# A ring for the keys and other memory for chunks of y in a one-core hybrid block

## The chip, the cores and the metric

The kernel runs on one core of a Trainium2 chip. The metric is the device time of one execution in microseconds (us). The core's engines work side by side and meet only at semaphores: TensorE (PE; its weight loads are shown as PEld), VectorE (DVE), ScalarE (ACT), GpSimd (POOL) and SyncE (SP), which here issues most of the DMAs; POOL issues the others. SBUF is the on-chip memory for operands, PSUM the one that TensorE writes.

## The reference

One layer of an autoregressive decoder for 1024 positions of width 1024, in float32:

```python
mod = c @ w_ada + b_ada                       # shift, scale, gate
h = rmsnorm(x, norm_g) * (1 + scale) + shift
proj = h @ w_in     # q, k, v, g_attn, xr, g_rnn, m_attn, m_rnn
y_attn = sliding_window_attention_with_sinks(rope(q), rope(k), v, sinks) * silu(g_attn)
y_rnn = rg_lru(causal_depthwise_conv(xr), ...) * silu(g_rnn)
merged = sigmoid(m_attn) * (y_attn @ w_attn_proj) + sigmoid(m_rnn) * (y_rnn @ w_rnn_proj)
x = x + gate * (merged @ w_out)
out = rmsnorm(x, final_g)
```

The attention has 16 query heads in 4 groups, each group with one key and value head of width 64. A block of 128 queries sees its own block of 128 keys and the one before, under a band mask of 128 positions, plus one learned sink value per head.

## The kernel before

**Numbers.** Each float32 operand of a matmul is split into a high part, its copy rounded to the matmul's format, and a low part, the rest. A product is the sum of high x high, low x high and high x low. So keys are stored as two parts per block (the axis `b` of `k_d`), weights as `wh` and `wl`, and y as `yh` and `yl`.

**The block products.** `w_in` is applied in pairs of 128-column chunks. Each pair takes seven products of half size in place of eight (a Strassen-like scheme): class `Pair`, with the list of steps in `run`. One step is a slot: 12 matmuls of 512 columns on TensorE. A slot's products read the normalised x (`hh`, `hl`) or sums and differences of its quarters (high parts `nh`, low parts `nl`). `make_operands` makes four tiles `nl`, one for each i from 0 to 3, each of 128 partitions x 2 x 1024. Each tile holds four quarters of 512 columns, which different products read: `NT1` is the first half of row 0, `NT3` the second half of row 0, `NT4` the first half of row 1, `T2` the second half of row 1. There are 23 pairs. `s_last`, the first slot of the last pair, is 154. The last pair reads `NT1` in slot 155, `T2` in slot 157, the quarters of `hh` and `hl` with numbers 4 to 7 in slots 158 and 159, `NT3` in slot 160 and `NT4` in slots 156 and 161.

**Memory.** Pools of tiles are opened and closed in the manner of a stack, from the left and from the right. `hb` (`hh` and `hl` 4 to 7), `hx` (first x transposed, later `nl`), `hn` (`nh`) and `stp` belong to `h_ctx`, and this is closed when `rp_steps` begins; `ypool`, `tout` and `hpool` then take over their memory. A tile in such memory waits, before it is first written, for the tiles that lay there.

**The attention loop** (line 1720, at the end of `tile_hybrid_block`) runs over u = 0 to 34. Each turn starts unit u (a group's block of 128 queries, four heads) and carries on the units before it: scores and maxima of u, exponentials of u - 1, transposes of u - 2, values of u - 3. Between the scores of u and the transposes stands one piece of other TensorE work from the generator `fill`: in units 0 to 5 the last slots 156 to 161 of the block products, from unit 6 on the pieces of `rp_steps`. A piece is 12 matmuls in either case.

**`rp_steps`** is the product of y (the recurrent branch's output, eight chunks of 128 rows, in DRAM as `yh_d` and `yl_d`) with `w_rnn_proj`. Its first eight pieces are for the output chunks 0 and 1 and read y in this order: chunks 6 and 7 (units 6 and 7), 4 and 5 (units 8 and 9), 0 and 1 (units 10 and 11), 2 and 3 (units 12 and 13). After these all chunks are in SBUF and are read again for the output chunks 2 to 7.

**Loads of y** (`load_y`). Chunk 6 and the high part of chunk 7 were left in SBUF. The low part of chunk 7 and all of chunk 0 go into halves of `hh` and `hl` 0 to 3; they are asked for in slots 157 and 159. Chunks 4 and 5 are asked for at the start of `rp_steps`, chunks 1, 2 and 3 in its pieces 1, 2 and 3, all into `ypool` (12 tiles of 512 KB). One chunk is 1 MB: a high and a low half of 512 KB.

**Loads of keys and queries** (`load_kq`, line 1319). Units 2m and 2m + 1 make pair m. Its tile `ks` holds three blocks of keys (the one before and its own two; only two at the start of a group), 384 KB, and `qs` its queries, 512 KB. Two pools take turns. Pair 0 is loaded early, in the middle of the last gates' work (line 1068), pair 1 in `open_attn`, and pair m, from 2 on, behind the scores of unit 2m - 3, whose pool it takes over.

**Gates** (`load_gq`, line 1549). A pair's attention output is multiplied by its gate, 256 KB from `ga_d`, loaded into the same six buffers `r` that the weight halves of `w_rp` use (`load_r`). Gate m is asked for at the end of unit 2m + 2, and `a_prep` multiplies two or more units later: in `f1` on DVE, `f2` on ACT, `f3` on DVE.

**Order.** Up to `order.close()` each engine issues its instructions in the order in which the program writes them; `at_slot` puts steps behind a slot's product. So SP's queue is in that order too: a DMA that must wait, such as a store whose data are not ready, holds all DMAs behind it. Stores made within the loop are set aside in `behind` and issued by `flush` after the unit's piece. Behind `order.close()` the instructions are placed by the compiler's scheduler.

Of the kernel before, what the change touches and what calls it, by code (L numbers as in the profile page):

```python
# [13 lines left out]
F32R = mybir.dt.float32r  # L14
# [4 lines left out]
ALU = mybir.AluOpType  # L19
# [3 lines left out]
P = 128  # L23
# [32 lines left out]
def tile_hybrid_block(ctx, tc, x, pk, rows, posr, posi, c_row, w_ss, w_gate, w_main, w_v,  # L56
# [8 lines left out]
    def f32(ap):  # L65
        return ap.bitcast(F32)
# [75 lines left out]


    hba = ctx.enter_context(tc.tile_pool(name="hba", bufs=1))
    h_ctx = ExitStack()
    hb = h_ctx.enter_context(tc.tile_pool(name="hb", bufs=1))
    b12_ctx = ExitStack()
# [10 lines left out]
                lst.append([a[:, SL[0]], a[:, SL[1]]])  # L158
                full.setdefault(kc, []).append(a[:])
    xx = b12_ctx.enter_context(tc.tile_pool(name="xx", bufs=1, side="right"))  # L160
    hx = h_ctx.enter_context(tc.tile_pool(name="hx", bufs=4))
    xall = [hx.tile([P, 2, S], F32, tag="X", name="xT") for i in range(3)]
    xall.append(xx.tile([P, 2, S], F32, name="xT3"))
    xT = [xall[kc % 4][:, kc // 4, :] for kc in range(KC)]
# [390 lines left out]
    B11 = [(hh[i][0], hl[i][0]) for i in range(4)]  # L555
    B21 = [(hh[i + 4][0], hl[i + 4][0]) for i in range(4)]
    B22 = [(hh[i + 4][1], hl[i + 4][1]) for i in range(4)]
    NT1, NT3, NT4, T2 = [], [], [], []

    def differences(i):  # L560
        b11, b12_ = xT[i][:, SL[0]], xT[i][:, SL[1]]
# [476 lines left out]
    def after_gates(hb, oc):  # L1038
# [22 lines left out]
        def d2():  # L1061
            V.tensor_tensor(out=t["it"][:], in0=t["it"][:], in1=W["xc", hb, oc][2][:],
                            op=ALU.mult)
            W["used", hb, oc] = True
            if c == KC - 1:
                xc_ctx.close()
                W["kq", 0] = pool(at_ctx, "kq0", side="right")
                load_kq(0)

        def a3():  # L1070
            A.activation(tl("th"), t["rz"][:], AF.Tanh)
# [230 lines left out]
    def open_attn():  # L1302
        nonlocal at, psx
        psm_ctx.close()
        psx = pool(psx_ctx, "psx", space=PSUM)
        W["kq", 1] = pool(at_ctx, "kq1", side="right")
        W["pp"] = pool(at_ctx, "pp", bufs=3, side="right")
        W["pp"].tile([P, 64], F32, name="pad", bufs=1)
        W["neg"] = W["pp"].tile([P, 8], F32, name="neg", bufs=1)
        G.memset(W["neg"][:], -1e30)  # L1310
        for nm in ("vb", "hl", "yo"):
            W[nm] = pool(at_ctx, nm, side="right")
        at = pool(at_ctx, "at", side="right")
        load_kq(1)
        for u in range(4):
            load_v(u)
            load_d(u)

    def load_kq(m):
        g, t0 = m // 4, (m % 4) * 256  # L1320
        ks = W["kq", m % 2].tile([P, 3, 2, P], F32R, tag="ks", name="ks")
        kv = k_d.rearrange("(p j) n b t -> j p n b t", j=4)[g]
        n0 = t0 // P
        lo = 1 if t0 == 0 else 0
        dma(ks[:, lo:, :, :], kv[:, n0 - 1 + lo:n0 + 2, :, :])
        qs = W["kq", m % 2].tile([P, 4, 256], F32R, tag="qs", name="qs")
        dma(qs[:], q_d[g][m % 4].rearrange("(a j) t -> a j t", j=4))
        U["kq", m] = ks, qs

    def load_v(u):  # L1330
        vb = U["v", u] = W["vb"].tile([P, P], F32R, tag="vb", name="vb", bufs=5)
# [11 lines left out]

    def scores(u):
        g, n = u // 8, u % 8
        ks, qs = U["kq", u // 2]
        qc = slice((n % 2) * P, (n % 2 + 1) * P)
        kb = n % 2 + (0 if n else 1)
        s_full = psx.tile([P, 1024], F32, tag="s", name="s_ps")
        s_ps = s_full[:].rearrange("p (j k) -> p j k", j=4)  # L1350
        for j in range(4):
            o = s_ps[:, j, :] if n else s_ps[:, j, P:]
            for b in range(2):
                W["pe"] = T.matmul(o, qs[:, j, qc], ks[:, kb:n % 2 + 2, b, :],  # L1354
                                   start=(b == 0), stop=(b == 1))
        sm = W["pp"].tile([P, 2, 4], F32, tag="small", name="small", bufs=4)
        U["s", u] = s_ps, U.pop(("p", u)), sm

    def maxima_a(u):
        s_ps, px, sm = U["s", u]  # L1360
        A.copy(px[:, :, 0:P], s_ps[:, :, P:])

    def maxima_d(u):
        s_ps, px, sm = U["s", u]
        p = px[:, :, 0:P]
        V.copy_predicated(p, W["mgt"][:].unsqueeze(1).to_broadcast([P, 4, P]),
                          s_ps[:, :, 0:P] if u % 8 else
                          W["neg"][:, 0:1].unsqueeze(1).to_broadcast([P, 4, P]))
        V.tensor_reduce(out=sm[:, 0, :], in_=px[:], axis=AX.X, op=ALU.max, negate=True)

# [97 lines left out]
                todo.pop(0)()  # L1468

    def load_y(c):  # L1470
        if c == 0:
            yh[c], yl[c] = [[t[i][0] for i in range(2)] for t in (hh, hl)]
            for i in range(2):
                dma(yh[c][i], yh_d[c][:, SL[i]])
                dma(yl[c][i], yl_d[c][:, SL[i]])
            return
        if c >= 6:
            yh[c], yl[c] = [[y_in[c, b][:, t_] for t_ in SL] if (c, b) in y_in else
                            [hh[2 + i][0] for i in range(2)] for b in range(2)]
            if c == 7:  # L1480
                for i in range(2):
                    dma(yl[c][i], yl_d[c][:, SL[i]])
            return
        h_ = W["yp"].tile([P, S], F32R, tag="Y", name="yh")
        l_ = W["yp"].tile([P, S], F32R, tag="Y", name="yl")
        dma(h_[:], yh_d[c])
        dma(l_[:], yl_d[c])
        yh[c] = [h_[:, SL[0]], h_[:, SL[1]]]
        yl[c] = [l_[:, SL[0]], l_[:, SL[1]]]

    def rp_steps():
        h_ctx.close()
        pb_ctx.close()
        psr = pool(ps_ctx, "psr", space=PSUM, side="right")
        rp_acc.extend(psr.tile([P, S], F32, name=f"rp{i}") for i in range(2))
        W["yp"] = pool(ctx, "ypool", bufs=12)
        W["tout"] = pool(ctx, "tout", bufs=1)
        W["hpool"] = pool(ctx, "hpool", bufs=6)

        def part(c, kc2):  # L1500
            for kc in (2 * kc2, 2 * kc2 + 1):
                W["pe"] = mm_k([rp_acc[c % 2][:, t] for t in SL], (O.get((c, 0)), O.get((c, 1))),
                               kc, xh=yh, xl=yl, ends=(6, 3) if c < 2 else (0, KC - 1))

        def finish(c):
            def f():
                flush()
                t = W["tout"].tile([P, S], F32, tag="rp", name="rp32")
                A.copy(t[:], rp_acc[c % 2][:])
                store(tr_d[c], t[:])  # L1510
            later_a.append(f)
            if "att" not in W:
                do_later()

        seq = [(c, k) for k in (3, 2, 0, 1) for c in range(2)]
        seq += [(c, k) for c in range(2, KC) for k in range(4)]
        load_y(4)
        load_y(5)
        for i, (c, k) in enumerate(seq):
            part(c, k)  # L1520
            if i in (1, 2, 3):
                load_y(i)
            if i in (1, 2):
                prep_r(i - 1, 0)
            if i in (6, 10):
# [160 lines left out]
    while W["slot"] < 7 * (len(pairs) - N_ATT) + 1:  # L1686
# [2 lines left out]

    s_last = 7 * len(pairs) - 7  # L1690
    load_y(6)
    at_slot(s_last + 2, ("N", 0, 0, lambda: load_r(0)), ("N", 0, 0, lambda: load_y(7)),
            ("N", 0, 0, lambda: load_r(1)), ("N", 0, 0, lambda: load_y(0)),
            ("N", 0, 0, lambda: prep_r(0, 1)), ("N", 0, 0, lambda: prep_r(1, 1)))

    def fill():
# [23 lines left out]
    for u in range(32 + 3):  # L1720
# [42 lines left out]
        do_later()  # L1763
        if u >= 3 and u % 2 == 0:
            late.append((u - 3) // 2)
        if u >= 2 and len(loaded) < 16 and len(loaded) <= (u - 2) // 2 and (
                len(loaded) - (late[0] if late else (u - 2) // 2) < 2):
            m = len(loaded)
            load_gq(m)
            loaded[m] = u  # L1770
# [62 lines left out]
    for c in range(KC):  # L1833
# [26 lines left out]
            A.copy(h, t[:, LEFT])  # L1860
            V.tensor_tensor(out=l, in0=t[:, LEFT], in1=f32(h), op=ALU.subtract)
        else:
            mh, ml = [ypool.tile([P, S], F32R, tag="Y", name=n_) for n_ in ("mh", "ml")]
            for i in SL:
                A.copy(mh[:, i], t[:, i])
            V.tensor_tensor(out=ml[:], in0=t[:], in1=f32(mh[:]), op=ALU.subtract)
            A12.append((mh[:, LEFT], ml[:, LEFT]))
            A22.append((mh[:, RIGHT], ml[:, RIGHT]))
            a11, a21 = [raw[c - 4][:, i] for i in SL]
# [227 lines left out]
```

## Time and profile before

| | us |
|---|---|
| median of 3 runs | 909.88 |
| lowest and highest run | 909.71, 911.13 |
| the profiled execution | 909.71 |
| its span from first to last instruction | 908.0 |
| first attention unit to the last piece of `rp_steps` on TensorE | 557.9 to 745.7 |

The profile's page gives the busy time of each engine as a share of the span. A matmul's end is modelled, so a busy TensorE need not be at its peak. The chain of waits is followed back from the last instruction to whatever released it; a row has a start, a duration, an engine or a DMA, a tile and the line of the code. The windows give the busy time of each engine in a stretch, the TensorE clock that was granted (1.00 is full), the mean busy share of the 16 DMA engines, and what they moved. A row of the DMA view has the tiles, the issuing queue, the count, the size of one, and the median time from issue to landing.

### The profile page before, as it was taken

How to read it: one execution, taken by the hardware profiler on the slowest of the kernel's cores; microseconds unless marked ns; L12 is line 12 of the kernel's file. 1: busy time of each engine (PE TensorE's matmuls, PEld its weight loads, DVE VectorE, ACT ScalarE, POOL GpSimd, SP SyncE). 2: the span in 40 equal slices, each digit the busy share in tenths (PEclk: the TensorE clock that was granted, in tenths of full speed). 3: DMA queues.
4: the chain of work that ended last, by engine and by line, in shares of the span. 5: the costliest groups of instructions: out<-in, count | busy, mean ns of one | idle time of the engine just before them, and what ended most of it. 6: DMA issues, size and time to landing. Idle time of an engine off the chain costs nothing.

```text
span 908.0 us, 12850 instructions
## 1 busy us (share of the span) xinstructions
PE 892.6 (98%) x4314; PEld 747.0 (82%) x4315; DVE 718.5 (79%) x1063; ACT 569.8 (63%) x1099; POOL 186.8 (21%) x330
## 2 busy tenths in 40 slices
PE   9999999999999999999999999997999999999997
PEld 6789888888888888888888888886888888888786
DVE  6998697989679877897897696996999836578855
ACT  7965564655566865777686974885888732115535
POOL 6430241200000000000000002695887720000000
PEclk9999999999999999999999999998999999999999
DMA  9829489863542374265534347997887379416604
GB/s 360 332 94 284 146 258 294 273 212 128 196 163 105 128 251 144 101 229 165 202 112 167 124 137 227 298 344 193 245 237 221 114 263 362 139 47 232 209 1 185
DMA packets 93829, 179.79 MB, mean 198 GB/s; under 512 B 15506, under 2 KB 36002, under 8 KB 93764
## 3 DMA queue, kind: packets, MB, share of 16 engines
q1 hardware_dynamic: 82336, 164.44, 53.0%
q0 software_dynamic: 11280, 14.27, 5.7%
q8 instruction: 34, 0.56, 0.3%
q14 instruction: 31, 0.25, 0.1%
q10 hardware_dynamic: 148, 0.27, 0.1%
HBM read 121.60 MB, written 57.64 MB: 197 GB/s over the span
## 4 chain that ended last, share of the span: by engine, by line
PE 89%; DMA 4%; DVE 3%; ACT 2%; issue 1%; SPq 0%; ACTq 0%
PE bk L714 48%; PE rp L175 13%; PE pgate L1031 5%; PE out L1900 4%; PE pmain L175 4%; PE s_ps L1354 3%; PE pmain L487 2%; PE bk L487 2%; PE pv L1424 2%; DMA yh<-yh_d 2%; DMA qs<-q_d 1%; PE pt L1388 1%; DMA wo<-wo_d 1%; PE pmain L1603 1%; PE pmain L1601 1%; PE pmain L1602 1%
## 5 line engine op out<-in xcount | busy, mean ns | idle before, releaser
L714 PE MATMUL bk<-nh,wh 128*128 128x512 f32 x368 | 143.3, 389 | 0.0
L714 PE MATMUL bk<-nl,wh 128*128 128x512 f32 x368 | 143.2, 389 | 0.0
L714 PE MATMUL bk<-nh,wl 128*128 128x512 f32 x368 | 98.4, 389 | 0.0
L106 ACT CAST wh<-r 128x512 fp32r<-128x512 f32 x107 | 65.5, 618 | 34.1 <-PE pmain L175 10.4
L112 DVE TENSOR_TENSOR wl<-r,wh 128x512 fp32r<-128x512 f32 x91 | 62.1, 691 | 26.2 <-ACT wh L106 26.1
L714 PEld LDWEIGHTS bk<-nh,wl 128*128 128x128 f32 x368 | 69.1, 188 | 14.3
L714 PEld LDWEIGHTS bk<-nl,wh 128*128 128x128 f32 x368 | 69.1, 188 | 14.3
L714 PEld LDWEIGHTS bk<-nh,wh 128*128 128x128 f32 x368 | 69.1, 188 | 14.2
L63 POOL DMA_DIRECT2D yl_d<-it x1 | 0.6, 568 | 349.7 <-DVE it L1114 349.7
L714 PE MATMUL bk<-hl,wh 128*128 128x512 f32 x184 | 71.6, 389 | 0.0
L714 PE MATMUL bk<-hh,wh 128*128 128x512 f32 x184 | 71.6, 389 | 0.0
L112 DVE TENSOR_TENSOR wl<-ws,wh 128x512 fp32r<-128x512 f32 x76 | 51.8, 684 | 6.8 <-ACT wh L106 6.8
L106 ACT CAST wh<-ws 128x512 fp32r<-128x512 f32 x76 | 45.9, 615 | 8.4 <-DVE ws L736 4.1
L1374 ACT ACTIVATE p<-p,small 128x129 f32<-128x129 f32 x128 | 50.0, 396 | 0.0
L714 PE MATMUL bk<-hh,wl 128*128 128x512 f32 x184 | 49.2, 389 | 0.0
L1354 PE MATMUL s_ps<-ks,qs 128*128 128x256 f32 (+1 forms) x256 | 36.5, 286 | 5.2 <-DMA qs<-q_d 5.2
L714 PEld LDWEIGHTS bk<-hl,wh 128*128 128x128 f32 x184 | 34.6, 188 | 7.2
L714 PEld LDWEIGHTS bk<-hh,wl 128*128 128x128 f32 x184 | 34.5, 188 | 7.2
L714 PEld LDWEIGHTS bk<-hh,wh 128*128 128x128 f32 x184 | 34.5, 188 | 7.1
L1354 PEld LDWEIGHTS s_ps<-ks,qs 128*128 128x128 f32 x256 | 33.6, 195 | 6.8 <-issue 5.6
L175 PE MATMUL rp<-yh,wh 128*128 128x512 f32 x112 | 35.8, 402 | 0.0
L714 PE MATMUL bk<-hha,wh 128*128 128x512 f32 x92 | 35.8, 389 | 0.0
(379 smaller groups left out, 2385.3 us busy)
## 6 DMA issues: line engine op xcount, KB each, us to landing
r<-w_main SPq DMA_DIRECT2D x100, 256.0 KB, 4.3
wada<-w_ss SPq DMA_DIRECT2D x16, 512.0 KB, 9.0
qs<-q_d SPq DMA_DIRECT2D x16, 512.0 KB, 8.0
wo_d<-wr SPq DMA_DIRECT2D x28, 256.0 KB, 4.3
wo<-wo_d SPq DMA_DIRECT2D x14, 512.0 KB, 6.6
ks<-k_d SPq DMA_DIRECT2D x12, 384.0 KB, 6.2
xt<-x SPq DMA_DIRECT2D x8, 512.0 KB, 6.9
sma_d<-c SPq DMA_DIRECT2D x16, 256.0 KB, 4.2
```

The source lines that it names most:

```text
L106: A.copy(dst[0][:], src)
L112: eng.tensor_tensor(out=dst[1][:], in0=src, in1=f32(dst[0][:]), op=ALU.subtract)
L175: mm = T.matmul(ps[hf], ww, xx[kc][hf], start=(kc == ends[0] and ww is w_h and xx is xh), stop=(kc == ends[1] and xx is xl))
L487: T.matmul(starts[c][hf], ww[:, c0:c0 + P], xh[kc][hf], start=(kc == 0 and t_ == "h"), stop=(kc == KC - 1 and t_ == "l"))
L714: W["pe"] = T.matmul(ps, ww[:, kc * P:(kc + 1) * P], b[kc][i], start=(first and n == 0), stop=(n == 11), skip_group_check=not first)
L1031: W["pe"] = T.matmul(ps[:, SL[hf]], ww[:, c0:c0 + P], xx_[:, SL[hf]], start=(ic == 0 and i == 0), stop=(ic == 1 and i == 2))
L1354: W["pe"] = T.matmul(o, qs[:, j, qc], ks[:, kb:n % 2 + 2, b, :], start=(b == 0), stop=(b == 1))
L1374: A.activation(px[:, j, :], px[:, j, :], AF.Exp, bias=sm[:, 0, j:j + 1], accum_out=sm[:, 1, j:j + 1])
L1388: W["pe"] = T.transpose(pt[:, :, j, :], px[:, j, 0:P], ident[:])
L1424: W["pe"] = T.matmul(pv[:, cols], w, t_[:, cols], start=(i == 0), stop=(i == len(m) - 1))
L1601: T.matmul(o, hh[kc][th][:, ts_], wh[:, cols], start=(kc == 0), stop=False)
L1900: T.matmul(o, a[k][x_][:, p * P:(p + 1) * P], b[k][y_][:, cols], start=(first and k == 0 and i == 0), stop=(k == 3 and i == 2), skip_group ...
```

## The change

- Keys lie in one tile `ks` of six blocks, used as a ring. Pair m brings only its own two blocks (256 KB); block number u lies at place u % 6. Where u % 6 is 0, the block before lies at place 5, so that the two blocks come in the other order; `cur_prev` tells which half of the scores belongs to which block.
- Queries get a pool of two tiles. The first pair's queries are now loaded in `open_attn`, ahead of the second pair's keys and queries.
- The pool `hx` stays open to the end, and the four tiles `nl` are kept in `NL`. Chunks 4 and 5 of y go as quarters of 256 KB into the parts of `nl` that belonged to `NT1` and `T2`, chunks 2 and 3 into those of `NT3` and `NT4`, which lie side by side. Only chunk 1 goes into `ypool`, which now has 4 tiles. Later `mh` and `ml` lie in `nl` too.
- The order of requests: chunk 7 and `r` of 0 in slot 156, chunk 4 in 157, `r` of 1 and chunk 5 in 158, chunk 0 in 159, chunk 1 at the start of `rp_steps`; chunks 2 and 3 as before.
- A gate is asked for at u >= 2m + 4 while u < 14, and from u = 14 on at u >= 2m + 2 as before.

```diff
@@
+    hx = ctx.enter_context(tc.tile_pool(name="hx", bufs=4))
...
-    hx = h_ctx.enter_context(tc.tile_pool(name="hx", bufs=4))
@@ make_operands
         nl = hx.tile([P, 2, S], F32R, tag="X", name="nl")
+        NL.append(nl)
@@ after_gates, d2
-                W["kq", 0] = pool(at_ctx, "kq0", side="right")
-                load_kq(0)
+                ring = pool(at_ctx, "ring", side="right")
+                W["ks"] = ring.tile([P, 6, 2, P], F32R, name="ks")
+                load_k(0)
@@ open_attn
-        W["kq", 1] = pool(at_ctx, "kq1", side="right")
+        W["qs"] = pool(at_ctx, "qs", bufs=2, side="right")
+        load_q(0)
...
-        load_kq(1)
+        load_k(1)
+        load_q(1)
@@
-    def load_kq(m):
...
+    def load_k(m):
+        n0, b0 = (m % 4) * 2, 2 * m % 6
+        kv = k_d.rearrange("(p j) n b t -> j p n b t", j=4)[m // 4]
+        dma(W["ks"][:, b0:b0 + 2, :, :], kv[:, n0:n0 + 2, :, :])
+
+    def load_q(m):
+        qs = U["q", m] = W["qs"].tile([P, 4, 256], F32R, tag="qs", name="qs")
+        dma(qs[:], q_d[m // 4][m % 4].rearrange("(a j) t -> a j t", j=4))
+
+    def cur_prev(u):
+        swap = u % 6 == 0
+        return [slice(i * P, (i + 1) * P) for i in ((0, 1) if swap else (1, 0))]
@@ scores
+        i = u % 6
+        kb = slice(0, 6, 5) if i == 0 else slice(i - 1, i + 1)
...
-                W["pe"] = T.matmul(o, qs[:, j, qc], ks[:, kb:n % 2 + 2, b, :],
+                W["pe"] = T.matmul(o, qs[:, j, qc], W["ks"][:, kb if n else slice(i, i + 1), b, :],
@@ load_y
+        if c == 1:
+            both = [W["yp"].tile([P, S], F32R, tag="Y", name="y") for _ in range(2)]
...
+        if c in (2, 3):
+            both = [NL[2 * c - 4 + b][:].rearrange("p a s -> p (a s)")[:, HALF:HALF + S]
+                    for b in range(2)]
+            yh[c], yl[c] = [[t[:, t_] for t_ in SL] for t in both]
+            for t, d in zip(both, (yh_d, yl_d)):
+                dma(t, d[c])
+            return
...
+        elif c >= 4:
+            yh[c], yl[c] = [[NL[2 * b + i][:, c - 4, SL[c - 4]] for i in range(2)]
+                            for b in range(2)]
...
+        for b, (t, d) in enumerate(((yh[c], yh_d), (yl[c], yl_d))):
+            if (c, b) not in y_in:
                 for i in range(2):
+                    dma(t[i], d[c][:, SL[i]])
@@ rp_steps
-        W["yp"] = pool(ctx, "ypool", bufs=12)
+        W["yp"] = pool(ctx, "ypool", bufs=4)
...
-        load_y(4)
-        load_y(5)
+        load_y(1)
...
-            if i in (1, 2, 3):
+            if i in (2, 3):
                 load_y(i)
@@
-    at_slot(s_last + 2, ("N", 0, 0, lambda: load_r(0)), ("N", 0, 0, lambda: load_y(7)),
-            ("N", 0, 0, lambda: load_r(1)), ("N", 0, 0, lambda: load_y(0)),
+    at_slot(s_last + 2, [ask_y(7), ask_r(0)], ask_y(4), [ask_r(1), ask_y(5)], ask_y(0),
@@ attention loop
-            load_kq(u // 2 + 2)
+            load_k(u // 2 + 2)
+            load_q(u // 2 + 2)
...
-        if u >= 2 and len(loaded) < 16 and len(loaded) <= (u - 2) // 2 and (
+        if u >= 2 and len(loaded) < 16 and len(loaded) <= (u - (4 if u < 14 else 2)) // 2 and (
@@ behind order.close()
-            mh, ml = [ypool.tile([P, S], F32R, tag="Y", name=n_) for n_ in ("mh", "ml")]
+            mh, ml = [NL[c - 4][:, a, :] for a in range(2)]
```

More of the change, by code (lines that the diff above doesn't have):

```diff
@@ L557, in tile_hybrid_block @@
     B22 = [(hh[i + 4][1], hl[i + 4][1]) for i in range(4)]
-    NT1, NT3, NT4, T2 = [], [], [], []
+    NT1, NT3, NT4, T2, NL = [], [], [], [], []
     def differences(i):
@@ L1317, in open_attn @@
             load_d(u)
-    def load_kq(m):
[L1320 to L1328, printed above, removed]
+    def load_k(m):
[8 more added lines that the diff above has]
+        return [slice(i * P, (i + 1) * P) for i in ((0, 1) if swap else (1, 0))]
     def load_v(u):
@@ L1345, in scores @@
         g, n = u // 8, u % 8
-        ks, qs = U["kq", u // 2]
+        qs = U["q", u // 2]
         qc = slice((n % 2) * P, (n % 2 + 1) * P)
-        kb = n % 2 + (0 if n else 1)
+        i = u % 6
+        kb = slice(0, 6, 5) if i == 0 else slice(i - 1, i + 1)
         s_full = psx.tile([P, 1024], F32, tag="s", name="s_ps")
@@ L1351, in scores @@
         for j in range(4):
-            o = s_ps[:, j, :] if n else s_ps[:, j, P:]
+            o = s_ps[:, j, :] if n else s_ps[:, j, cur_prev(u)[0]]
             for b in range(2):
-                W["pe"] = T.matmul(o, qs[:, j, qc], ks[:, kb:n % 2 + 2, b, :],
+                W["pe"] = T.matmul(o, qs[:, j, qc], W["ks"][:, kb if n else slice(i, i + 1), b, :],
                                    start=(b == 0), stop=(b == 1))
@@ L1360, in maxima_a @@
         s_ps, px, sm = U["s", u]
-        A.copy(px[:, :, 0:P], s_ps[:, :, P:])
+        A.copy(px[:, :, 0:P], s_ps[:, :, cur_prev(u)[0]])
     def maxima_d(u):
@@ L1366, in maxima_d @@
         V.copy_predicated(p, W["mgt"][:].unsqueeze(1).to_broadcast([P, 4, P]),
-                          s_ps[:, :, 0:P] if u % 8 else
+                          s_ps[:, :, cur_prev(u)[1]] if u % 8 else
                           W["neg"][:, 0:1].unsqueeze(1).to_broadcast([P, 4, P]))
@@ L1470, in load_y @@
     def load_y(c):
[L1471 to L1475, printed above, removed]
+        if c == 1:
+            both = [W["yp"].tile([P, S], F32R, tag="Y", name="y") for _ in range(2)]
+            yh[c], yl[c] = [[t[:, t_] for t_ in SL] for t in both]
+            for t, d in zip(both, (yh_d, yl_d)):
+                dma(t[:], d[c])
+            return
+        if c in (2, 3):
+            both = [NL[2 * c - 4 + b][:].rearrange("p a s -> p (a s)")[:, HALF:HALF + S]
+                    for b in range(2)]
+            yh[c], yl[c] = [[t[:, t_] for t_ in SL] for t in both]
+            for t, d in zip(both, (yh_d, yl_d)):
+                dma(t, d[c])
             return
@@ L1479, in load_y @@
                             [hh[2 + i][0] for i in range(2)] for b in range(2)]
-            if c == 7:
-                for i in range(2):
[L1482 to L1489, printed above, removed]
+        elif c >= 4:
+            yh[c], yl[c] = [[NL[2 * b + i][:, c - 4, SL[c - 4]] for i in range(2)]
+                            for b in range(2)]
+        else:
+            yh[c], yl[c] = [[t[i][0] for i in range(2)] for t in (hh, hl)]
+        for b, (t, d) in enumerate(((yh[c], yh_d), (yl[c], yl_d))):
+            if (c, b) not in y_in:
+                for i in range(2):
+                    dma(t[i], d[c][:, SL[i]])
     def rp_steps():
@@ L1691, in tile_hybrid_block, with ask_y, ask_r @@
     load_y(6)
-    at_slot(s_last + 2, ("N", 0, 0, lambda: load_r(0)), ("N", 0, 0, lambda: load_y(7)),
-            ("N", 0, 0, lambda: load_r(1)), ("N", 0, 0, lambda: load_y(0)),
+    def ask_y(c):
+        return "N", 0, 0, lambda: load_y(c)
+    def ask_r(c):
+        return "N", 0, 0, lambda: load_r(c)
+    at_slot(s_last + 2, [ask_y(7), ask_r(0)], ask_y(4), [ask_r(1), ask_y(5)], ask_y(0),
             ("N", 0, 0, lambda: prep_r(0, 1)), ("N", 0, 0, lambda: prep_r(1, 1)))
@@ L1862, in tile_hybrid_block @@
         else:
-            mh, ml = [ypool.tile([P, S], F32R, tag="Y", name=n_) for n_ in ("mh", "ml")]
+            mh, ml = [NL[c - 4][:, a, :] for a in range(2)]
             for i in SL:
                 A.copy(mh[:, i], t[:, i])
-            V.tensor_tensor(out=ml[:], in0=t[:], in1=f32(mh[:]), op=ALU.subtract)
+            V.tensor_tensor(out=ml, in0=t[:], in1=f32(mh), op=ALU.subtract)
             A12.append((mh[:, LEFT], ml[:, LEFT]))
```

## The prediction

> **What bounds the kernel now.** I read the page's shares first, then the chain of waits that ended last, then who waited for whom.
>
> ```profile
> span 908.0 us, 12850 instructions
> PE 892.6 (98%) x4314; PEld 747.0 (82%) x4315; DVE 718.5 (79%) x1063; ACT 569.8 (63%) x1099; POOL 186.8 (21%) x330
> PE s_ps L1354 <- DMA qs<-q_d: 5.2, 1, 5.2
> ```
>
> TensorE is busy for 98% of the span, so only its idle time and its slow time can be won. The last row, from TensorE's waits, is the one long wait: the scores of some unit waited 5.2 us for a query tile. The chain tells where.
>
> ```profile
> 557.91 0.84 PE s_ps L1354 x8
> ...
> 583.72 0.96 PE s_ps L1354 x8
> ...
> 590.42 14.90 DMA yh<-yh_d
> 605.34 12.88 DMA qs<-q_d
> 618.35 2.05 PE s_ps L1354 x8
> 620.40 4.38 PE rp L175 x12
> ...
> 625.93 0.96 PE s_ps L1354 x8
> 626.88 2.75 PE rp L175 x12
> 630.78 0.95 PE s_ps L1354 x8
> ...
> 664.74 0.96 PE s_ps L1354 x8
> ```
>
> Each `s_ps` row is the start of one unit (8 score matmuls); 557.91 is unit 0. Counting on, 583.72 is unit 6, the first that carries a piece of `rp_steps`, 618.35 is unit 12, and 664.74 is unit 21. A query tile asked for at 605.34 landed at 618.2. Before it on the chain stands a chunk of y that took 14.90 us: transfers were queueing. After the wait TensorE is also slow for a while: 12 `rp` matmuls take 4.38 us instead of 2.75.
>
> What the wait costs, slow time included, is read from two stretches of the same work. Units 6 to 13 and 14 to 21 each hold seven units of one pattern (eight units to a group of heads). They take 625.93 - 583.72 = 42.21 us and 664.74 - 630.78 = 33.96 us. So **8.25 us** is the most that this place can give.
>
> The windows say what was short: columns are stretch, its length, busy time of PE, PEld, DVE, ACT, POOL, then the granted TensorE clock, the DMA share and GB/s.
>
> ```profile
> 540.00:555.00 15.00, 15.00 (x68) 12.42 (x67) 12.19 (x19) 7.37 (x13) 5.75 (x12) 1.00 0.88 270
> 562.00:580.00 18.00, 18.00 (x107) 15.76 (x106) 15.75 (x29) 14.70 (x49) 4.92 (x12) 1.00 0.84 277
> 580.00:590.00 10.00, 10.00 (x63) 8.75 (x62) 9.19 (x16) 9.63 (x30) 9.53 (x16) 1.00 0.92 304
> 590.00:600.00 10.00, 9.87 (x60) 8.50 (x60) 9.61 (x18) 8.94 (x29) 9.49 (x17) 1.00 1.05 359
> 600.00:608.00 8.00, 8.00 (x49) 6.95 (x48) 7.68 (x14) 6.82 (x24) 7.54 (x14) 1.00 1.06 340
> 608.00:618.00 10.00, 5.17 (x31) 4.19 (x29) 8.46 (x16) 5.92 (x18) 7.73 (x14) 0.95 1.06 285
> 640.00:714.00 74.00, 73.95 (x455) 64.99 (x454) 69.94 (x124) 63.81 (x201) 59.08 (x105) 1.00 0.73 217
> ```
>
> From 580 to 618 the DMA engines are full (share 0.92 to 1.06), while from 562 to 580 they have 16% left and from 640 on 27%. In those 38 us they moved 3.04 + 3.59 + 2.72 + 2.85 = 12.2 MB, 0.321 MB/us. The wait is a matter of bytes in this stretch. From 640 to 714 the loop runs with no idle TensorE, so the same loop needs nothing else.
>
> **The change, part by part.** First, y's chunks 4 and 5 leave the full stretch. SP's own requests, from its timeline (start, issue time, tile), show what is in it.
>
> ```profile
> 579.85 0.32 SPq L63 DMA_DIRECT2D ks<-k_d  x1
> 580.22 0.42 SPq L63 DMA_DIRECT2D qs<-q_d  x1
> 580.70 0.42 SPq L63 DMA_DIRECT2D yh<-yh_d  x1
> ...
> 582.44 1.72 SPq L63 DMA_DIRECT2D yl<-yl_d  x1
> ...
> 605.34 0.32 SPq L63 DMA_DIRECT2D qs<-q_d  x1
> ```
>
> From 579.85 to 605.34 SP asks for keys of 256 + 384 + 384 KB, queries of 3 x 512, ten half chunks of y of 512, two gates and two halves of `w_rp` of 256 each: 8704 KB. Afterwards four of the ten halves of y (chunks 4 and 5) are gone, and the keys are 3 x 256 KB; the number of gates in the stretch stays at two, as each comes one pair later. That is 6400 KB, or 2304 KB (2.36 MB) less; at 0.321 MB/us **7.35 us** less. The query tile of unit 12 would land at 618.2 - 7.35 = 610.9. Unit 12 stood ready at 618.35 - 5.18 = 613.2 (the 5.18 us are the 5.2 of the waits). So bytes alone hide it with 2.3 us to spare. SP's order helps further: requests that stood behind full queues (the 14.90 us of the chain) go out earlier. Chunks 1, 2 and 3 keep their places, ahead of that query tile, and so land ahead of it; chunks 2 and 3 are first used by unit 12's piece, chunk 1 by unit 10's. Their new memory is free early enough: the third and fourth quarters of the low parts are last read by the products of slots 160 and 161, units 4 and 5, which end before unit 6 at 583.72, and SP reaches chunk 2 behind unit 7.
>
> Second, chunks 4 and 5 now move in units 1 and 2, and there the earlier queries must still come in time.
>
> ```profile
> 562.25 0.38 SPq L63 DMA_DIRECT2D ga_d<-c  x1
> 562.73 0.91 SPq L63 DMA_DIRECT2D hha<-yl_d  x2
> ...
> 564.16 0.42 SPq L63 DMA_DIRECT2D qs<-q_d  x1
> ...
> 569.65 0.38 SPq L63 DMA_DIRECT2D ga_d<-c  x1
> ...
> 573.66 0.43 SPq L63 DMA_DIRECT2D qs<-q_d  x1
> ```
> ```profile
> qs<-q_d SPq DMA_DIRECT2D x1, 512.0 KB, 8.0
> ```
>
> The last row is from the DMA view of 573.2 to 573.9: the query tile for unit 6 took 8.0 us to land, so it came at 581.7, and unit 6 needs it at 583.7. From 562.25 up to it SP asks for 4608 KB: a store of 256, chunk 7's two quarters, keys and queries of 896, `w_rp` 512, a store, a gate, chunk 0's 1024, keys and queries of 896. Afterwards it is 5632 KB: eight quarters of chunks 4 and 5 (2048 KB) come in; chunk 7 (512, now asked for ahead of the blocked store), the gate (256, two units later) and 2 x 128 KB of keys go out. The added 1024 KB (1.05 MB) take 3.3 us at 0.321 MB/us if nothing hides them; the 16% of 18 us that the engines were idle hide 2.9 us. The tile lands between 581.7 and 585.0, at 582.1 if the idle time is used, against 583.7: a new wait of 0 to 1.3 us. I take **0.3 us**, near the lower end, because the quarters are asked for at the head of the stretch, where SP otherwise stands still behind the store of 569.65. The tile of unit 4, asked for at 564.16, gets 384 KB more ahead of it, 1.2 us; unit 4 starts some 10 us after that request, and 8.0 us were enough for the later tile.
>
> The Trainium skill speaks against the quarters: "DMA: Bandwidth & Descriptors", Rules for kernel authors, asks for at least 1 MiB in one DMA, and its table (section Bandwidth) gives 138 GB/s for 64 KB and 341 for 1 MB. Between them 256 KB might run at some 240 GB/s, an estimate from that page; the 2.1 MB of quarters would then need 8.7 us instead of 6.5, and unit 6 would wait some 2 us more. The trace disagrees: in this window, with quarters of chunk 7, halves of `w_rp` and one query tile in flight, it has 353 GB/s at a share of 0.98.
>
> ```profile
> 565.00:570.00 5.00, 5.00 (x33) 4.42 (x32) 4.08 (x9) 4.37 (x14) 0.19 (x1) 1.00 0.98 353
> ```
>
> Third, the first query tile moves from SP's requests near 515 to `open_attn`.
>
> ```profile
> 543.22 0.41 SPq L63 DMA_DIRECT2D ks<-k_d  x1
> ```
>
> It stands first there, at some 543.2, and unit 0 needs it at 557.9. Keys and queries asked for at this place grow from 896 to 1280 KB, 1.31 MB, 4.9 us at the 270 GB/s of that window; even the 12.88 us of the worst tile above would make it 556.1. Cost nothing; the cover is 1.8 to 9.8 us. The pool that it lies in spans what the second pair's pool spans now, whose loads at 543.22 did not wait.
>
> Fourth, the ring. The number of score matmuls and their shapes are the same; only addresses change, and in one unit of six the two blocks lie five apart. No row shows such a stride: I bound it by the 0.84 and 0.96 us of the score rows, i.e. nothing, to twice that in four units, 4 us, and take nothing, as the moving data of these matmuls already come in pieces of 128 elements. A keys load now waits only for the unit that last read its two blocks, one unit earlier than today; the queries right behind it wait for what they wait now.
>
> Fifth, gates later: the product with the gate (DVE L1561, ACT L1566, DVE L1571) moves one unit back for pairs 1 to 5 and is level again from unit 17 on. The work is the same. DVE is at 94.5% from 640 to 714 (69.94 of 74) without a wait of TensorE; one unit that carries it twice is some 1.6 us denser. Zero to 0.5 us; I take nothing. Sixth, `ypool` shrinks by what `hx` now keeps, so the rest lies as tightly as before; the code behind the hand-written order may be placed anew, which I put at 0.5 us either way and at zero in the sum.
>
> What stays of the 8.25 us: TensorE also waited for POOL in that stretch, and POOL (9.5 of 10 us busy there) keeps its work.
>
> ```profile
> 589.77 0.30 PEld L175 LDWEIGHTS rp<-yh,wl 128*128 128x128 f32 x2 [0.21 <-POOL wl L112]
> 593.17 0.19 PEld L1424 LDWEIGHTS pv<-pm,vd 128*128 128x128 f32 x1 [0.34 <-POOL pm L1410]
> ```
>
> I leave 0.5 us for it. The sum is -8.25 + 0.5 + 0.3 = -7.45 us. The profiled execution took 909.71 us around its span of 908.0, and the median of the runs is 909.88: **902.3 us**.
>
> **The rivals.** One: the wait moves to unit 6. For it: only 2.0 us of slack today. The worst case above is 1.3 us; if in addition SP stands in front of chunk 4 until the product of slot 157 is done (should a whole low-part tile count as in use), it begins at 565.2 instead of 562.7 and all behind it is 2.5 us later. That gives a wait of up to 3.8 us and times of 903.5 to 906. Or the quarters move more slowly than whole halves: at the 277 GB/s of 562 to 580, taken as their limit, the 2.1 MB need 1.1 us more than at 0.321 MB/us, and unit 6 waits that long: 903.4, with 0.03 of this rival's 0.16. By the rule of the Trainium skill above this is the case to expect.
>
> Two: half of the wait at unit 12 stays, because requests in flight and not bytes limit the queue, or because POOL's small transfers take what is freed: some 4 us of the 8.25, 906 to 907.5. Against it: 353 to 359 GB/s where the queue is full.
>
> Three: nothing is won, as the next late tile takes the place (unit 14's queries, or y). Both stand in the same queue, behind or beside the tile of unit 12, and come sooner by the same 7.35 us, so little speaks for it: 908 to 911.
>
> Four, the slower side: the ring counts as one tile, so each unit that opens a pair waits for the newest keys, which themselves wait for the unit before.
>
> ```profile
> 588.41 1.12 PE L1354 MATMUL s_ps<-ks,qs 128*128 128x256 f32 x8
> 593.87 1.00 PE L1354 MATMUL s_ps<-ks,qs 128*128 128x128 f32 x8
> ks<-k_d SPq DMA_DIRECT2D x12, 384.0 KB, 6.2
> ks<-k_d SPq DMA_DIRECT2D x4, 256.0 KB, 5.0
> ```
>
> Between one unit's scores (end 589.53) and the next (593.87) lie 4.3 us, and keys take 5.0 to 6.2 us to land: 0.7 to 1.9 us for each of 14 pairs, 10 to 27 us, or some 920 us in all. It decides from 0.53 us a pair on (7.45 / 14). No row speaks against it directly; the loads and the matmuls name separate ranges of the ring, which makes it the less likely way.
>
> **How the numbers follow.** Forecast (wait gone, 901.2 to 903.5) 0.70; unit 6 waits 0.16; half stays 0.06; nothing won 0.04; slower 0.04. The range goes from 901.2, where the POOL waits and the 0.3 us go too and the end is placed a little better, to 905.8, nearly all of rival one; it leaves out 0.15 and the edges of the first two. About 0.2% (1.8 us) is what a measurement of this kernel tells from no change: faster 0.92, the same 0.04, slower 0.04.
>
> **What would show it.** Right: no wait of the scores for a query tile over 1 us; a full clock (1.00) where 608 to 618 has 0.95; some 34 us from unit 6 to unit 13; a DMA share near 1 from 562 on and below 1 by 605; the keys at 256 KB in all 16 loads. Wrong: a wait of unit 6's scores (rival one), of unit 12's (two), or a wait for keys at every second unit (four). The forecast falls if the queue was not full because of bytes.

## The result and the profile after

| | before | changed |
|---|---|---|
| median of 4 runs each, us | 910.1 | 902.32 |
| lowest and highest, us | 909.71, 911.13 | 902.17, 903.36 |
| profiled execution, us | 909.71 | 902.32 |
| its span, us | 908.0 | 900.6 |

The ratio is 0.992 (95% interval 0.9908 to 0.9932). The forecast was 902.3 us. The page of the changed kernel, and TensorE's longest waits:

```profile
span 900.6 us, 12871 instructions
PE 889.9 (99%) x4314; PEld 744.8 (83%) x4315; DVE 718.8 (80%) x1063; ACT 569.5 (63%) x1099; POOL 189.2 (21%) x330
```
```profile
PE bk L258 <- DVE warm L260: 1.4, 1, 1.4
PE bk L487 <- ACT hha L413: 0.9, 2, 0.7
PE out L1919 <- ACT out L1964: 0.5, 1, 0.5
```

The ratio is the changed kernel's time over that of the kernel before. The wait of 5.2 us for a query tile is gone and nothing of its size has come in its place. TensorE's busy time fell by 2.7 us with the same number of matmuls: that is the slow time behind the wait, 4.38 - 2.75 us of the 12 `rp` matmuls and 2.05 - 0.96 us of the scores themselves. The chain of waits around the place (start, us, what):

```profile
609.34 2.75 PE rp L175 x12
612.09 0.44 PE pt L1395 x4
612.52 0.47 PE pv L1431 x2
613.00 1.22 PE s_ps L1361 x8
614.21 2.75 PE rp L175 x12
...
618.11 0.96 PE s_ps L1361 x8
```

613.00 is unit 12 and 618.11 is unit 13: no DMA stands between them and the 12 `rp` matmuls take 2.75 us. SP's requests in its timeline show what moved.

```profile
562.52 0.90 SPq L63 DMA_DIRECT2D nl<-yh_d  x2
563.52 0.86 SPq L63 DMA_DIRECT2D nl<-yl_d  x2
...
566.55 1.11 SPq L63 DMA_DIRECT2D nl<-yh_d  x2
568.11 0.99 SPq L63 DMA_DIRECT2D nl<-yl_d  x2
...
575.35 0.32 SPq L63 DMA_DIRECT2D qs<-q_d  x1
...
580.03 0.42 SPq L63 DMA_DIRECT2D y<-yh_d  x1
580.50 0.42 SPq L63 DMA_DIRECT2D y<-yl_d  x1
...
595.21 0.32 SPq L63 DMA_DIRECT2D ks<-k_d  x1
599.66 0.32 SPq L63 DMA_DIRECT2D qs<-q_d  x1
```

The first four rows are chunks 4 and 5 as quarters, the two `y` rows chunk 1. The query tile of unit 12 is asked for at 599.66, as soon as unit 9's scores (598.51 to 599.63) have freed its memory; it was 605.34 before, and unit 9's scores had freed its memory at 599.81 there. What held it is seen among SP's own waits in the kernel before, from 579 to 606 (us in total, times, longest):

```profile
SPq L63 <- DMA yl<-yl_d: 4.0, 2, 2.3
SPq L63 <- DMA yh<-yh_d: 3.3, 3, 1.6
```

These are waits for the landing of other tiles. In all 14 traces, wherever the landing is known, none of SP's requests goes out before the request eight places ahead of it has landed. In the kernel before, the one eight places ahead of unit 12's queries is the chunk of y of 590.42, which landed at 590.42 + 14.90 = 605.32. In the changed kernel it had landed at 597.6. So fewer bytes in the queue bring this tile sooner in two ways: its request goes out 5.7 us earlier, and it takes 10.2 us in place of 12.9.

The windows have the columns of those shown before:

```profile
562.00:580.00 18.00, 18.00 (x106) 15.72 (x106) 15.75 (x30) 14.87 (x50) 5.12 (x12) 1.00 0.93 335
575.00:580.00 5.00, 5.00 (x33) 4.41 (x32) 4.80 (x10) 3.56 (x13) 3.56 (x9) 1.00 1.05 407
580.00:590.00 10.00, 10.00 (x63) 8.72 (x62) 9.19 (x16) 9.65 (x30) 9.53 (x16) 1.00 1.07 313
590.00:600.00 10.00, 9.87 (x61) 8.50 (x60) 9.57 (x18) 8.31 (x28) 9.45 (x18) 1.00 1.04 333
600.00:608.00 8.00, 8.00 (x50) 7.00 (x49) 7.61 (x14) 6.53 (x23) 7.58 (x13) 1.00 1.01 313
608.00:618.00 10.00, 10.00 (x61) 8.48 (x60) 9.57 (x17) 8.54 (x28) 7.31 (x13) 1.00 0.72 205
```

From 562 to 580 the engines now move 335 GB/s in place of 277, and from 608 on they have room (0.72 in place of 1.06). Between them they are still full.

The DMA views of the two critical query tiles, of unit 12 (asked for at 599.66) and of unit 6 (at 575.35), in this order:

```profile
qs<-q_d SPq DMA_DIRECT2D x1, 512.0 KB, 10.2
```
```profile
qs<-q_d SPq DMA_DIRECT2D x1, 512.0 KB, 6.8
```

Unit 12's tile landed at 609.9, 3.1 us before the unit could start; unit 6's at 582.1, 1.2 us before (unit 6's scores start at 583.36).

### The profile page after: what moved, and what is told of

Its sections match the earlier page's. It is cut to its first block, busy times and chain, and to the rows that moved or that the text cites. A ratio compares the mean times of both kernels' runs of the same rounds, so it can differ in the third digit from the quotient of the medians.

```text
span 900.6 us, 12871 instructions
## 1 busy us (share of the span) xinstructions
PE 889.9 (99%) x4314; PEld 744.8 (83%) x4315; DVE 718.8 (80%) x1063; ACT 569.5 (63%) x1099; POOL 189.2 (21%) x330
## 4 chain that ended last, share of the span: by engine, by line
PE 90%; DVE 3%; ACT 2%; DMA 2%; POOL 1%; issue 1%; POOLq 0%; ACTq 0%
PE bk L715 49%; PE rp L175 14%; PE pgate L1032 5%; PE out L1919 4%; PE pmain L175 4%; PE s_ps L1361 3%; PE pv L1431 2%; PE pmain L487 2%; PE bk L487 2%; PE pt L1395 1%; DMA wo<-wo_d 1%; PE pmain L1613 1%; PE pmain L1615 1%; PE pmain L1614 1%; ACT jk L1937 1%
## 5 line engine op out<-in xcount | busy, mean ns | idle before, releaser
L175 PE MATMUL rp<-nl,wh 128*128 128x512 f32 x128 | 37.3, 393 | 0.0
L715 PE MATMUL bk<-hla,wh 128*128 128x512 f32 x92 | 35.8, 389 | 0.0
```

Of the source, the lines that this page charges most:

```text
L175: mm = T.matmul(ps[hf], ww, xx[kc][hf], start=(kc == ends[0] and ww is w_h and xx is xh), stop=(kc == ends[1] and xx is xl))
L715: W["pe"] = T.matmul(ps, ww[:, kc * P:(kc + 1) * P], b[kc][i], start=(first and n == 0), stop=(n == 11), skip_group_check=not first)
```

## The experiments

In the table, "unit 0 to 13" is the time on TensorE between the first score matmuls of units 0 and 13, from the timeline. It leaves out the start and the end of the kernel. The wait is the scores' longest in the profiled execution, and in brackets the unit. Runs that stand side by side are from one chip; the kernel before had 909.12 beside e1 to e4, 909.23 beside e5 to e7, 909.1 beside e8 to e10 and 908.8 beside e11 and e12.

| run | what | unit 0 to 13, us | wait, us | median, us | ratio to before (95%) |
|---|---|---|---|---|---|
| before | | 68.01 | 5.2 (12) | 910.1 | |
| changed | | 60.40 | none | 902.32 | 0.992 (0.9908 to 0.9932) |
| e8 | the same again | 60.31 | none | 902.29 | 0.9931 (0.9916 to 0.9946) |
| e1 | chunks 4 and 5 late | 64.82 | 2.6 (12) | 907.57 | 0.998 (0.9969 to 0.9991) |
| e2 | three blocks of keys | 60.55 | 0.6 (6) | 902.29 | 0.9923 (0.9909 to 0.9938) |
| e3 | gates early | 60.44 | 0.3 (6) | 902.85 | 0.9929 (0.9916 to 0.9943) |
| e4 | e2 and e3 together | 62.19 | 1.5 (6) | 903.21 | 0.9932 (0.9917 to 0.9947) |
| e5 | 1 MB copied besides | 65.79 | 4.0 (12) | 906.36 | 0.9966 (0.995 to 0.9981) |
| e6 | 2 MB copied besides | 70.47 | 5.7 (12) | 912.16 | 1.0031 (1.0019 to 1.0043) |
| e7 | stores by SP | 60.98 | 1.3 (12) | 902.8 | 0.9923 (0.9908 to 0.9937) |
| e9 | stores by SP, one unit later | 59.72 | none | 902.51 | 0.9928 (0.9912 to 0.9943) |
| e10 | chunk 5 late | 60.38 | none | 902.7 | 0.9934 (0.9919 to 0.9949) |
| e11 | e9 again | 61.90 | 2.2 (12) | 901.99 | 0.9922 (0.9904 to 0.994) |
| e12 | chunk 5 late, and e4 | 61.45 | 1.1 (12) | 903.82 | 0.9946 (0.993 to 0.9963) |

The theory: unit 12 waited because too many bytes stood ahead of its query tile in a stretch in which the DMA engines are full, and taking chunks 4 and 5 out of it is what pays. The rivals: the order of the requests on SP, the ring, or the later gates.

### Chunks 4 and 5 back where they were (e1)

```diff
-    at_slot(s_last + 2, [ask_y(7), ask_r(0)], ask_y(4), [ask_r(1), ask_y(5)], ask_y(0),
+    at_slot(s_last + 2, [ask_y(7), ask_r(0)], [], ask_r(1), ask_y(0),
...
-        load_y(1)
+        load_y(4)
+        load_y(5)
...
-            if i in (2, 3):
+            if i in (1, 2, 3):
```

> The changed kernel with chunks 4 and 5 asked for where they were before, at the start of rp_steps, and chunk 1 again behind piece 1; their memory, the ring and the late gates stay. Theory (bytes): 2048 KB come back into the full stretch, 6.5 us at 0.321 MB/us. Unit 12's query tile, which landed at 609.9 against a need at 613.0, would land near 616.4: a wait of about 3.4 us and a slow clock behind it, 905.7 to 908.4 us. Rival (the order of requests on SP, not bytes, made it late): the whole wait is back, 909 to 911 us. Rival (the ring and the gates did it): 902 to 903 us.

TensorE's waits and the chain in e1:

```profile
PE s_ps L1361 <- DMA qs<-q_d: 2.6, 1, 2.6
```
```profile
605.11 11.00 DMA qs<-q_d
616.11 0.14 issue
616.24 1.39 PE s_ps L1361 x8
617.64 4.11 PE rp L175 x12
```

The wait of unit 12 is back, at 2.6 us with a slow TensorE behind it, and the time is 5.3 us above the changed kernel's: inside the band of the bytes, with a shorter wait than the 3.4 us expected. The tile's request goes out at 605.11, again just behind the landing of the one eight places ahead (593.24 + 11.80 = 605.04). The number of requests alone is not what counts: e1 asks for chunks 4 and 5 in eight requests, where the kernel before had four, and its tile comes sooner. What is left of the change without chunks 4 and 5, a ratio of 0.998, is about a quarter of the gain, which strikes out the reading that the ring and the gates bring most of it.

### The ring and the gates undone (e2, e3, e4)

e2 takes `load_kq` and the scores of the kernel before in place of the ring; e3 has one line:

```diff
-        if u >= 2 and len(loaded) < 16 and len(loaded) <= (u - (4 if u < 14 else 2)) // 2 and (
+        if u >= 2 and len(loaded) < 16 and len(loaded) <= (u - 2) // 2 and (
```

e4 has both.

> The changed kernel with keys and queries as before: three blocks for a pair in two pools, the first pair's queries early. Theory: only 2 x 128 KB more in the stretch, 0.8 us of 3.1 us to spare; no wait of the scores, 902.3 us, within 0.4 us. Rival (a keys load that waits for one unit less is what helped): unit 12 waits again, 904 us or more.

> The changed kernel with the gates asked for two units earlier, as before. Theory: 256 KB more ahead of unit 12's queries, 0.8 us of 3.1 us to spare, 902.3 us within 0.4 us, no wait. Rival (SP stands still for a free buffer r, and the queue behind it is late): a wait at unit 12 or 6 of 1 to 3 us, 903.5 to 905.5 us.

> The changed kernel with both undone: three blocks for a pair and early gates; what is left of the change is y's chunks in the low parts. Theory: 512 KB more ahead of unit 12's queries, 1.6 us of 3.1 us to spare, still no wait: 902.3 us, within 0.6 us. So the place of chunks 4 and 5 alone carries the gain. Rival (all three parts are needed): a wait of 1 us or more at unit 6 or 12, 903.5 us or more.

None of the three makes unit 12 wait, as expected. But all three make unit 6 wait, where each theory had no wait. In e4 the wait is the one of its rival (over 1 us at unit 6), though the median of 903.21 stays under that rival's 903.5. TensorE's timeline rows of unit 6's scores, first e2, then e3, then e4:

```profile
584.11 1.19 PE L1355 MATMUL s_ps<-ks,qs 128*128 128x256 f32 x8 [0.57 <-DMA qs<-q_d]
```
```profile
583.62 1.19 PE L1361 MATMUL s_ps<-ks,qs 128*128 128x256 f32 x8 [0.32 <-DMA qs<-q_d]
```
```profile
586.05 1.19 PE L1355 MATMUL s_ps<-ks,qs 128*128 128x256 f32 x8 [1.55 <-DVE plc L1400]
```

The last row names a DVE instruction, but in e4 unit 6's query tile was asked for at 577.51 and took 8.4 us: it landed at 585.9, 0.14 us before the scores, the same distance as in e1's chain. It is the DMA again. So the smaller keys and the later gate, 256 KB each ahead of unit 6's queries, pay at unit 6: without one of them 0.6 or 0.3 us, without both 1.5 us. In the whole time this is at most 0.9 us (903.21 against 902.29 to 902.32), and the ratios' intervals overlap, so it is shown by the waits of one execution each and not by the times; e4's profiled execution is the slowest of its six (904.69).

### More bytes in the full stretch (e5, e6)

```diff
+            if i == 2:
+                for x_ in range(2):
+                    dma(spare[x_], (yh_d, yl_d)[x_ % 2][4 + x_ // 2])
             if i in (2, 3):
                 load_y(i)
```

e6 has `range(4)`. The copies go from DRAM to DRAM and are not read.

> The changed kernel with two copies of 512 KB more, from y's memory to spare memory in DRAM, asked for by SP ahead of chunk 2 in unit 8. Theory: 1 MB more takes 3.3 us at 0.321 MB/us, just what unit 12's queries had to spare (3.1 us): a wait of 0 to 0.5 us, 902.3 to 902.9 us. If a copy costs the DMA engines less or more than a load, this moves. Rival (the time hangs on the order of requests, not on bytes): unchanged 902.3 us here and with twice as much.

> The same with four copies, 2 MB more in the full stretch. Theory: 6.5 us more, 3.1 of them hidden: unit 12 waits some 3.4 us and the clock falls for a while, 905.7 to 908.4 us, the same as with chunks 4 and 5 put back. Rival (order, not bytes): 902.3 us.

Both lost much more than expected: e5 4.0 us (its runs lie between 902.82 and 909.36), e6 9.8 us. Unit 12's scores in e5 and e6:

```profile
617.04 2.04 PE L1362 MATMUL s_ps<-ks,qs 128*128 128x256 f32 x8 [3.97 <-DMA qs<-q_d]
```
```profile
619.86 2.05 PE L1362 MATMUL s_ps<-ks,qs 128*128 128x256 f32 x8 [5.67 <-DMA qs<-q_d]
```

One MB of copies turned 3.1 us to spare into a wait of 4.0 us, 7.1 us, where 3.3 were expected. In e6 a wait of 1.0 us for `vd` comes on top. The direction is the theory's, and the rival by which only the order counts falls; but a copied MB is not a loaded MB, so this is no measure of the load's price. For that the next two runs put loads back.

### Half the dose, and three quarters (e10, e12)

```diff
-    at_slot(s_last + 2, [ask_y(7), ask_r(0)], ask_y(4), [ask_r(1), ask_y(5)], ask_y(0),
+    at_slot(s_last + 2, [ask_y(7), ask_r(0)], ask_y(4), ask_r(1), ask_y(0),
...
+        load_y(5)
         load_y(1)
```

e12 is this together with e4. For them the changed kernel was run again as e8, which gave what the result has.

> The changed kernel as it is, on the same chip as the next two, as their measure. Theory: a ratio of 0.992 to the kernel before, as in the result; no wait of the scores at unit 12, at most some tenths at unit 6.

> The changed kernel with chunk 5 alone asked for where it was before, at the start of rp_steps, ahead of chunk 1; chunk 4 stays early. Theory (bytes): half of the first experiment's dose, 1024 KB or 3.3 us, against the 3.1 us that unit 12's queries had to spare: a wait of 0 to 0.5 us there, none at unit 6; 902.3 to 903.5 us, far under half of the first experiment's loss of 5.3 us. Rival (each MB in the stretch costs its 3 us at once, nothing to spare): 905 us.

> The changed kernel with chunk 5 late, three blocks for a pair, and early gates: chunk 4 alone is moved out of the full stretch. Theory (bytes): 1536 KB come back, between the doses of e10 (1024 KB, no wait) and e1 (2048 KB, a wait of 2.6 us): 4.9 us at 0.321 MB/us against 2.7 to 3.1 us to spare, so unit 12 waits 1.8 to 2.2 us; by the 2.3 us that the dose of e10 took it would be 0.4 to 0.8 us. No wait at unit 6, whose queries have nothing of chunk 5 ahead of them. 903 to 906 us. Rival (only y's chunks matter, keys and gates do not): as e10, 902.7 us and no wait.

The DMA views of unit 12's queries in e10 (asked for at 601.77) and in e12 (at 603.20):

```profile
qs<-q_d SPq DMA_DIRECT2D x1, 512.0 KB, 10.5
```
```profile
qs<-q_d SPq DMA_DIRECT2D x1, 512.0 KB, 11.5
```

e10's tile landed at 612.3, 0.5 us before unit 12 was ready; e12's at 614.7, 1.0 us after it (with the start of the scores behind it, the wait of 1.1 us in the table). No wait at unit 6 in either. So e10 is as its theory had it, and its rival falls, like that of e12, whose wait lies between the two estimates of its theory. Put in a row, the KB put back and the time by which the tile came early or late: 0 KB, 3.1 and 2.7 us early (two executions); 1024 KB, 0.5 early; 1536 KB, 1.1 late; 2048 KB, 2.6 late. That is some 2.6 us for each 1024 KB, a little less than the 3.3 us from 0.321 MB/us.

This is a trend and not a price. e2, with only 256 KB of keys more, has its tile at 612.6 (asked for at 600.20, 12.4 us to land), 0.5 us early like e10; in e4, with 512 KB more, it came 4.3 us early, in part since unit 6's wait had moved unit 12 back. And the kernel of e9 had no wait in one execution and one of 2.2 us in another (below). The kernel before (2304 KB) would be 3.3 late on the trend and was 5.2. It differs from e1 by the three blocks, the early gates and the memory of chunks 2 to 5; whether one of these or the scatter makes the 1.9 us was not taken apart.

### POOL's stores (e7, e9, e11)

What is left in the changed kernel between units 6 and 13 is 34.59 - 33.96 = 0.6 us over the later pattern; TensorE waits there for POOL, with the stores of the last pair (`smr_d`) in front:

```profile
588.26 1.30 POOL L112 TENSOR_TENSOR wl<-r,wh 128x512 fp32r<-128x512 f32 x1
589.50 0.65 POOL L1348 COPY p<-pk_t 128x4 f32<-128x4 f32 x1
589.60 0.30 PEld L175 LDWEIGHTS rp<-yh,wl 128*128 128x128 f32 x2 [0.24 <-POOL wl L112]
590.09 1.10 POOL L63 DMA_DIRECT2D smr_d<-c  x2
591.20 1.27 POOL L1417 TENSOR_SCALAR_AFFINE_SELECT pm<-phc 64x256 fp32r<-64x256 f32 x2
592.53 0.89 POOL L1417 TENSOR_SCALAR_AFFINE_SELECT pm<-plc 64x256 fp32r<-64x256 f32 x2
593.00 0.19 PEld L1431 LDWEIGHTS pv<-pm,vd 128*128 128x128 f32 x1 [0.34 <-POOL pm L1417]
```

e7 lets SP issue them, e9 lets SP do so one unit later:

```diff
-                        own_stores.append(lambda: dma(dst[j][:, SL[th]], t["t"], G))
+                        own_stores.append(lambda: dma(dst[j][:, SL[th]], t["t"]))
```

> The changed kernel with the last pair's four stores of smr asked for by SP in place of POOL. Theory: POOL issues three of them (1.66 us of its time) just ahead of the weights' low part and the masks on which TensorE waits 0.24 + 0.34 us in units 7 and 8; without them both waits go: 901.7 us, 0.6 less. Rival (POOL is behind by more than that, or SP's queue is held up by the stores): 902.3 us or more.

> The changed kernel with the last pair's four stores of smr asked for by SP one unit after their data are made, so that SP does not stand still for them. Theory: with the stores right behind the unit SP stood until 584.5 and 589.7 for ScalarE's tanh, and all loads behind came 5 us late; one unit later it does not, POOL has its 1.66 us, and the waits of 0.24 + 0.34 us in units 7 and 8 go: 0.6 us less than the changed kernel beside it, and no wait for unit 12's queries. Rival (POOL's time is not what these units wait for): the same time as the changed kernel.

> The kernel of e9 once more. There TensorE went from unit 0 to unit 13 in 59.72 us, 0.6 less than the changed kernel beside it (60.31), but its first 90 us took 1.2 us longer, and the whole time was the same. Theory: the longer start is chance (the kernels are the same there) and varies from run to run: unit 0 to 13 again in 59.7 us, and a time of 901.3 to 902.6 us according to the start. Rival: the start is always longer in this kernel, unit 0 again at 558.9 us.

In e7 the POOL waits are gone, but SP stood still for ScalarE's tanh. ScalarE's timeline, then SP's:

```profile
583.87 0.62 ACT L828 ACTIVATE c<-c 128x512 f32<-128x512 f32 x1
```
```profile
584.51 0.32 SPq L63 DMA_DIRECT2D smr_d<-c  x1
584.89 0.42 SPq L63 DMA_DIRECT2D y<-yh_d  x1
```

Chunk 1, asked for at 580.03 in the changed kernel, goes out 4.9 us later, and unit 12 waits 1.3 us: the rival of e7's expectation. e9 mends that: 59.72 us from unit 0 to unit 13, 0.6 less than e8, as expected, and no wait. Yet the time is not better than the changed kernel's, since unit 0 starts at 558.9 in e9's profiled execution and at 557.6 to 557.7 in the changed kernel's two. In e11 it starts at 558.8, as its rival had it; unit 12's queries were asked for only at 603.96 there, and unit 12 waited 2.2 us. (The row of that wait names a DVE instruction, as in e4; the last part of the tile landed at 615.65, 0.13 us before the scores.)

The granted clock tells where the longer start comes from. The windows from 24 to 28 us, first of e8, then of e9:

```profile
24.00:28.00 4.00, 3.57 (x13) 2.47 (x14) 3.78 (x6) 3.97 (x7) 3.69 (x5) 1.00 1.04 406
24.00:28.00 4.00, 3.79 (x9) 2.77 (x10) 3.84 (x8) 3.97 (x8) 3.67 (x5) 0.57 1.04 408
```

Some 0.8 of the 1.2 us are lost before, in the first 19 us, where TensorE's first 12 matmuls take 5.30 us in e9 and 4.65 in e8; the rest is lost here. The same stretch has 0.57 in e11, and 0.57 to 0.68 in e1, e4, e7 and e12, whose unit 0 starts at 557.9 to 559.0; the other eight executions have 1.00, and unit 0 at 557.1 to 557.8. Two executions do not show that the start is always longer in e9's kernel: e9's five runs fall into two near 901.3 and three near 902.6, 1.2 us apart, and the profiled one is of the later group. What decides between the two starts stays open.

Less the wait, units 6 to 13 take 33.91 us in e7, e9 and e11 alike, against 34.50 in e8. So the gain of 0.6 us inside the loop is real, but the whole times (e11's six runs go from 900.81 to 904.79) do not tell these kernels from the changed one.

## Why the prediction was right

**The 8.25 us at unit 12.** Units 6 to 13 took 34.59 us in place of 42.20 by the timeline's starts, so 7.6 of the 8.25 us came. The 0.5 us left for POOL measured 0.6, the same two waits (0.24 and 0.34 us against 0.21 and 0.34), and e9 shows that they are POOL's.

**Bytes.** Unit 12's tile was to land at 610.9 by bytes alone and landed at 609.9, against a need at 613.0. The term of chunks 4 and 5 was 2048 of 2304 KB: e1 gives 5.3 us of the gain back, e10 with half the dose nothing that can be told from the scatter. The prediction named SP's order as a help beside the bytes; the requests show that it is the larger part of the way in which the bytes act. Of the 8.4 us by which the tile came sooner, 5.7 are the earlier request and 2.7 the shorter transfer. Rival two had requests in flight as the limit. There is one, of eight, but with fewer bytes in the queue the eight landed sooner, and no half of the wait stayed. As a price, 3.3 us for 1024 KB was above the 2.6 of the trend, and no single figure fits all runs.

**Unit 6.** Its tile was to land at 582.1, which is what it did. The 0.3 us in the sum were not needed. The step was right to see 0 to 1.3 us of risk there: e2 to e4 show waits of 0.3 to 1.5 us as soon as the keys and gates taken out in front are put back. The prediction counted both out of the bytes ahead of unit 6, but did not say that this is where the ring and the gates earn their place, and not at unit 12.

**The quarters.** The Trainium skill ("DMA: Bandwidth & Descriptors", Rules for kernel authors) asks for 1 MiB in one DMA; here eight and then four quarters of 256 KB stood in the queue and the engines moved 335 GB/s from 562 to 580 and 407 GB/s from 575 to 580. The rule's case, a later unit 6, did not come. (The other case of rival one, at 277 GB/s, comes to 1.0 us by its own figures, where the prediction has 1.1.)

**The ring.** Rival four, the slower side, fell: the keys asked for at 595.21 took 12.9 us to land, and units 9 and 10 started their scores in that time (598.51 and 603.37), so a load into the ring does not hold the units that read its other blocks. No unit waited for keys, and all 16 loads have 256 KB. Unit 6, whose two blocks lie five places apart, takes the same 1.12 us for its scores as before.

**The first queries.** They went into `open_attn` without a wait, as the unit 0 row of 557.55 shows (557.75 before).

**The sum** was -7.45 us and the profiled executions differ by 7.39. That the two agree to 0.1 us is luck: 0.2 us came from an earlier unit 0, and behind unit 21 the changed kernel took 0.4 us longer (243.84 against 243.43). Beside e8 the two medians differ by 6.8 us, in the result by 7.8. One sign was off: the DMA share was to be below 1 by 605, and is so only from 608 on (1.01 from 600 to 608). That did no harm, as the tile had been asked for 5.7 us earlier.

## What to carry to other kernels

When one wait in a loop is for a load, add up the bytes that were asked for ahead of it in the stretch where the DMA share is near 1, and look for a transfer among them that could start in an earlier stretch with room; memory that dies early, even quarters of larger tiles, is where it can land. Look also at what the late load's own request stood behind: here most of the gain was that it went out earlier. Then check the next deadline in front of that stretch in the same way, as the moved bytes now stand ahead of it. A store that waits for its data in an in-order queue can cost more than the engine time it frees.

## What the runs showed that was not expected

**Copies from DRAM to DRAM** cost more than loads: 1 MB of copies made unit 12's tile 7.1 us later in the profiled execution, 1024 KB of loads 2.2 to 2.6 us (medians 4.0 and 0.4 us above the changed kernel's).

**A short wait can slow the matmuls behind it.** After waits of 1.1, 1.3, 1.5 and 2.2 us the next 12 `rp` matmuls took 2.75 us. After the 2.6 us of e1 they took 4.11, after 4.0 us (e5) 3.39, after 5.2 us (the kernel before) 4.38 and after 5.7 us (e6) 4.71. The chain in e11, whose wait was 2.2 us, and then the windows from 616 to 624 of the kernel before, e1 and e11, with the granted clock as the third number from the end:

```profile
615.78 1.19 PE s_ps L1361 x8
616.97 2.75 PE rp L175 x12
```
```profile
616.00:624.00 8.00, 5.65 (x18) 4.87 (x19) 3.12 (x6) 2.65 (x10) 2.91 (x4) 0.57 0.94 244
616.00:624.00 8.00, 7.76 (x40) 6.82 (x41) 4.09 (x8) 3.36 (x12) 4.00 (x8) 0.79 0.71 191
616.00:624.00 8.00, 8.00 (x49) 7.05 (x49) 6.02 (x12) 5.36 (x17) 5.86 (x12) 1.00 0.40 126
```

So the four waits up to 2.2 us cost only themselves, and e1's 2.6 us cost 4.5 in the loop (64.82 - 60.31). With one execution for each length, this does not show that the length alone decides. The Trainium skill ("TensorE: Matmul & The Clock Gate", Part 1) has the clock fall to half after an idle window of some 3.4 us; here 2.6 us were enough in one execution.
